# A gated Fourier and attention block: order and rooms of the last gates' side work, clearing of the score rooms, and where the output weights are prepared

## The chip, the cores and the metric
One core of a Trainium2 chip runs the whole block as one program. The metric is the device time of one execution in microseconds (us), here the median of three. The engines are TensorE (PE in the rows, PEld its weight loads), VectorE (DVE), ScalarE (ACT), GpSimd (POOL) and SyncE (SP), which issues most transfers (DMAs). Each takes its own instructions strictly in order.

## The reference
```python
D_MODEL, SEQ, CTX_LEN, NA_HEADS, HEAD_DIM = 1024, 2048, 256, 8, 64
WIN_ROWS, WIN_COLS, D_FF = 8, 16, 4096
...
def fourier_mix(u):
    ug = u.reshape(b, n, N_FOURIER_GROUPS, FOURIER_GROUP_DIM)          # 4 groups of 128 channels
    return jnp.fft.fft2(ug, axes=(1, 3), norm="ortho").real
...
        sc = jnp.concatenate([s_loc, s_ctx], axis=-1)                  # window of 8 x 16 and the 256 context keys
        p = jax.nn.softmax(sc, axis=-1)
...
def gated_merge(h, y_four, y_attn, w_gate, w_fo, w_ao, w_o):
    gates = jax.nn.sigmoid(h @ w_gate)
    g_f, g_a = jnp.split(gates, N_BRANCHES, axis=-1)
    merged = g_f * (y_four @ w_fo) + g_a * (y_attn @ w_ao)
    return merged @ w_o
```
Before it stand a normalisation with scale and shift (from c and c_ctx) and one projection of the tokens to f, q, k, v; behind it a residual, a second normalisation and a squared-ReLU MLP. All is float32 in the reference.

## The kernel before
Most products are made of float16 halves: a factor is split into a high part H and the rest L, and three matmuls (HH, HL, LH) add up in PSUM. Splitting takes one ScalarE pass and one VectorE pass (`pair_of`, L374/L375 or L847/L848 in the rows), or three POOL passes (`parts_on_pool`, L1429 to L1433).

The stages, with times from the trace: normalisation and first projections to about 140 us; pairs of projections (`run_pair`: f, gates, q, v, k) to about 849; the Fourier transform over the sequence (`psq`) to 886; attention with work beside it to about 1230; output projection (`po`) and the MLP to the end at 2648.

A scheduler places the instructions of each engine from the program's order and modelled times. Two things bind it: `tc.issue_after(i)` keeps what is built inside it behind instruction i, and a tile's room (a tag with `bufs` copies) is taken again only when its last reader is done. Generators are run piece by piece beside a main stream: `next(side)` builds one more piece.

**Last gates.** In the last pair (two gate units, matmuls `ps_g`, evictions `ot_g` on ScalarE, stores `gT`) the side generator is `fourier_prep`. It loads the four Fourier groups fT (tile X, 1 MB each), takes their squares' sum on ScalarE (L932, written into the `fold` tile), folds them on POOL and VectorE, adds the sum over partitions on TensorE (`pfe`), and makes the channel transform (`pc`, evicted to gH/gL). In between it loads 8 MB of weights for their norms (tiles wn, a 1 MB load each, ScalarE square L892; two of the norms, in weights of the Fourier output, are added up by matmul `pw`), and adds and splits two sets of rows of the Fourier output weights (wf, wx). `tick` hands out the pieces by a `pace`. After the gates, `pss`, `pr` and `puc` make the row of frequency 0, and `psq` transforms over the sequence; its results are split into y0H/y0L and y1H/y1L.

**Ramp of the attention.** Bias tiles bt are loaded by SP and POOL and scaled on POOL (L1194). A head's block runs score matmuls `sc`, a VectorE pass that adds the bias, writes s and takes the maximum m (L1347), ScalarE's exponential (L1351), transposes `tp`, a split into pH and pL (L1363, L1368), and `pv`. The four rooms s (128 x 832) are set to zero once, on POOL (L1268). Meanwhile `mgs` and `vsc` (scales of the merge, chains of small VectorE instructions around the matmuls `pym` and `pyb`) are made.

**Beside the attention and at its end.** Fillers run between blocks: `merge_fourier` (matmuls `pmf`, results stored to mF), then `load_wa` (the attention's output weights wa), then `attn_out(0, ...)`: loads of the attention's result (`yat`, split to yaH and yaL), matmuls `pua`, gate products in `ga` and `ft`, and the merged halves mH, mL. `output_weights` (generator `gating`) loads and converts wo on POOL. What is left over runs when the attention is done, `attn_out(1, ...)` included. The parts touched here are driven by these lines:
```python
        if n >= 8 and n % 2:
            with tc.issue_after(last_qk[0].ins):
                next(gating, None)
```


## Time and profile before
| what | value |
|---|---|
| median of 3 executions (lowest to highest) | 2649.96 us (2649.69 to 2651.73) |
| the profiled execution: its time, its span | 2649.84 us, 2648.1 us |
| mean granted TensorE clock | 0.985 |
| TensorE busy | 2518.0 us, 95% |
| VectorE, ScalarE, POOL busy | 1815.2, 1165.6, 475.5 us |
| mean DMA rate over the span | 191 GB/s |

The span is what the profile covers; the execution's own time is 1.74 us longer. Times in rows count from the span's start. A row of a timeline has start, duration, engine, line, operation, out<-in, shape, count (xN: neighbours joined), and in brackets the idle time of that engine before it with the instruction or transfer that ended it. Granted clock 1.00 is full speed of TensorE, 0.50 half.

### The profile page before, as it was taken

The page shows a single profiled execution, that of the slowest core. Times are in us where ns is not written, and L with a number is a line of the kernel's source. Part 1 is how long each engine was busy: PE and PEld are TensorE (multiplying, and loading weights), DVE is VectorE, ACT ScalarE, POOL GpSimd, SP SyncE. Part 2 cuts the span into 40 slices and gives each one's busy share as a digit, 9 for nine tenths or more (in the row PEclk, how much of TensorE's full clock was granted, in tenths as well). Part 3 has the DMA queues.
Part 4 walks back from the last instruction along what each step waited for, and adds up shares of the span by engine and source line. Part 5 has one row for each costly group of instructions (what it writes and reads, how often), then busy time and mean ns, then how long its engine had stood idle before and what let it go on. Part 6 is the DMA issues. An engine that isn't in the chain of part 4 may idle for free.

```text
span 2648.1 us, 42112 instructions
## 1 busy us (share of the span) xinstructions
PE 2518.0 (95%) x15839; PEld 1446.4 (55%) x15839; DVE 1815.2 (69%) x3730; ACT 1165.6 (44%) x2078; POOL 475.5 (18%) x587
## 2 busy tenths in 40 slices
PE   7899989899989599988999999999999999999999
PEld 5445757767745377876665444444444444444444
DVE  7656986685535488886776697979877644546367
ACT  5523226453243288883444564637361423314050
POOL 1201111012111664373000121121211100000000
PEclk9899999999989799999999999999999999999999
DMA  7456689763193655655667677786776533333334
GB/s 280 138 200 207 194 276 324 243 213 122 59 289 111 169 148 165 181 134 187 228 229 281 245 253 243 248 271 222 279 241 225 176 96 108 99 105 102 102 101 155
DMA packets 223196, 506.38 MB, mean 191 GB/s; under 512 B 31804, under 2 KB 85828, under 8 KB 207888
## 3 DMA queue, kind: packets, MB, share of 16 engines
q1 hardware_dynamic: 189936, 384.53, 45.3%
q0 software_dynamic: 26272, 87.95, 9.5%
q10 hardware_dynamic: 6784, 31.21, 3.5%
q8 instruction: 124, 2.03, 0.3%
q14 instruction: 80, 0.66, 0.1%
HBM read 366.22 MB, written 137.38 MB: 190 GB/s over the span
## 4 chain that ended last, share of the span: by engine, by line
PE 71%; DVE 10%; DMA 8%; issue 4%; POOL 3%; ACT 3%; SPq 0%; ACTq 0%; DVEq 0%; POOLq 0%
PE p L85 21%; PE pm L85 18%; PE ps_g L85 8%; PE po L85 6%; DMA w12m<-in_w_mlp 3%; PE pua L85 3%; PE ps_k L85 2%; PE tp L1360 2%; PE ps_f L85 2%; PE pmf L1298 2%; PE pv L1374 1%; PE sc L1338 1%; DVE wo L375 1%; PE ps_q L85 1%; DMA raw<-in_w_mlp 1%
## 5 line engine op out<-in xcount | busy, mean ns | idle before, releaser
L85 PE MATMUL pm<-hc,wb 128*128 128x512 f16 x2688 | 582.6, 379 | 5.7 <-DVE u L1652 3.5
L85 PE MATMUL p<-wb,a 128*128 128x512 f16 x2688 | 581.9, 379 | 2.1 <-DVE X L1652 1.5
L85 PEld LDWEIGHTS <-wb 128*128 128x128 f16 x2688 | 263.0, 98 | 323.6 <-issue 7.4
L85 PEld LDWEIGHTS <-a 128*128 128x128 f16 x2688 | 263.0, 98 | 319.7 <-issue 2.9
L85 PE MATMUL ps_g<-hx,w_g 128*128 128x512 f16 x1536 | 347.3, 383 | 1.0 <-DVE qn_q L563 1.0
L1652 DVE TENSOR_TENSOR X<-X,p 128x512 f32<-128x512 f32 x280 | 184.2, 684 | 171.3 <-PE p L85 152.1
L85 PEld LDWEIGHTS <-hx 128*128 128x128 f16 x2304 | 226.7, 99 | 37.7 <-issue 5.3
L85 PEld LDWEIGHTS <-w_g 128*128 128x128 f16 x1536 | 151.8, 100 | 170.8 <-issue 7.0
L85 PE MATMUL po<-wo,mH 128*128 128x512 f16 x512 | 152.4, 379 | 2.8 <-DVE ga L1418 2.8
L1652 DVE TENSOR_TENSOR u<-pm,u 128x512 f32<-128x512 f32 x128 | 87.5, 689 | 84.3 <-PE pm L85 82.5
L1347 DVE CUSTOM_DVE_ANT_0 s<-sc,bt,qsc 128x736 f32<-128x736 f32 (+5 forms) x128 | 111.2, 869 | 46.4 <-PE sc L1341 21.8
L374 ACT ACTIVATE wo<-ws,msc 128x512 f16<-128x512 f32 x96 | 69.0, 718 | 166.9 <-DVE ws L415 131.6
L1656 ACT ACTIVATE p<-pm 128x512 f32<-128x512 f32 x32 | 18.9, 590 | 239.7 <-PE pm L85 239.7
L1368 DVE SCALAR_TENSOR_TENSOR pL<-tp,pH 128x640 f16<-128x640 f32 (+1 forms) x128 | 112.3, 877 | 11.4 <-ACT pH L1363 10.7
L1351 ACT ACTIVATE s<-s,m 128x736 f32<-128x736 f32 (+5 forms) x128 | 104.4, 816 | 35.6 <-DVE m L1347 35.2
L1786 POOL DMA_DIRECT2D xr<-x1d x32 | 17.3, 540 | 569.2 <-DVE X L1652 562.6
L501 ACT ACTIVATE ot_g<-ps_g,usc_g 128x512 f32<-128x512 f32 x64 | 43.5, 682 | 152.9 <-PE ps_g L85 139.6
L374 ACT ACTIVATE wo<-raw,msc 128x512 f16<-128x512 f32 x128 | 87.5, 709 | 40.3 <-DVE raw L415 18.5
L1360 PE MATMUL tp<-ident,s 128*128 128x128 f32 x704 | 103.6, 282 | 0.9 <-ACT s L1351 0.8
L375 DVE SCALAR_TENSOR_TENSOR wo<-raw,msc,wo 128x512 f16<-128x512 f32 x128 | 94.4, 747 | 8.0 <-ACT wo L374 8.0
L85 PE MATMUL po<-wo,mL 128*128 128x512 f16 x256 | 97.0, 379 | 0.0
L85 PE MATMUL pua<-yaH,wa 128*128 128x256 f16 x512 | 87.2, 272 | 9.6 <-DVE ga L1418 4.4
(562 smaller groups left out, 4403.7 us busy)
## 6 DMA issues: line engine op xcount, KB each, us to landing
wb<-w1d SPq DMA_DIRECT2D x224, 256.0 KB
wb<-w2d SPq DMA_DIRECT2D x224, 256.0 KB
w12m<-in_w_mlp SPq DMA_DIRECT2D x32, 1024.0 KB
raw<-in_w_mlp ACTq DMA_DIRECT2D x24, 1024.0 KB
w1d<-wo POOLq DMA_DIRECT2D x84, 256.0 KB, 3.8
w2d<-wo POOLq DMA_DIRECT2D x84, 256.0 KB, 4.0
gT<-ot_g SPq DMA_DIRECT2D x64, 256.0 KB
hc<-hcd SPq DMA_DIRECT2D x14, 1024.0 KB
```

What stands on the lines that cost most here:

```text
L85: last_mm[0] = pe.matmul(ps, l, r, start=(start and i == 0), stop=(stop and i == n - 1))
L374: act.activation(hi, src, AF.Copy, scale=scale)
L375: dve.scalar_tensor_tensor(out=lo, in0=src, scalar=scale, in1=hi, op0=ALU.mult, op1=ALU.subtract)
L501: act.activation(o, ps, func, scale=scale)
L1298: pe.matmul(ps, l, r, start=(i == 0), stop=(i == len(prods) - 1))
L1338: pe.matmul(sc[:, lo:lo + nl], q, k[:, k0:k0 + nr * 64].rearrange("p (r c) -> p r c", c=64)[:, :, c0:c0 + ncl], start=(i == 0), stop=(i == 1))
L1347: tail["dve"] = dve.tensor_tensor_reduce(out=s[:, :n], in0=sc, in1=bias, op0=ALU.add, op1=ALU.min, scale=qsc[:, 4:5], scalar=3.0e38, accum ...
L1351: tail["act"] = act.activation(s[:, :n], s[:, :n], AF.Exp, bias=m1[:, 0:1], scale=-1.0, accum_out=m1[:, 1:2])
L1360: tail["pe"] = pe.transpose(tp[:, i * 128:(i + 1) * 128], s[:, o:o + 128], ident)
L1368: tail["dve"] = dve.scalar_tensor_tensor(out=pL[:, :c], in0=tp[:, :c], scalar=PTOP, in1=pH[:, :c], op0=ALU.mult, op1=ALU.subtract)
L1374: tail["pe"] = pe.matmul(pv, p_[:nk, i * 128:(i + 1) * 128], vv[:nk, h2 * 128 + o:h2 * 128 + o + 64], start=(j == 0 and i == 0), stop=(j = ...
L1652: last["dve"] = dve.tensor_tensor(out=o, in0=x, in1=y, op=op)
```

## The change
In the last gates `fourier_prep` is written out in one fixed order of steps. Its tiles become fixed rooms: two for the rows (both, mix), one for the weights whose norms are taken, and two for the Fourier groups, of which the first shares the tag of the gates' raw weights. The next norm load follows the square of the one before. In the last pair each step is kept behind the last gate eviction on ScalarE (`last_out`), and `pace` is 8 instead of 6. Three DMAs of four rows go from POOL's to SyncE's queue. The pieces `pss`, `pr`, `puc` come to lie between gate matmuls.

The score rooms are cleared by VectorE. The loads and conversions of wo leave the attention's main loop: two, later three steps follow the stores of each of merge_fourier's eight outputs. wa is split on ScalarE and VectorE out of tiles that held the Fourier results y; ft of the second row block is multiplied on POOL.

The old `fourier_prep` is among the functions printed above; of its removed lines the diff shows none.

```diff
     def tick(share):
 
         ticks[0] += pace[0]
-        with tc.issue_after(last_load[0].ins):
+        with tc.issue_after(last_load[0].ins), tc.issue_after(last_out[0].ins) if side not in beside else nullcontext():
             while ticks[0] >= 2:
                 ticks[0] -= 2
...
-        act.activation(o, ps, func, scale=scale)
+        last_out[0] = act.activation(o, ps, func, scale=scale)
...
-        pace[0] = 6 if n == len(seq) - 1 else (0, 3, 2)[min(n, 2)]
+        pace[0] = 8 if n == len(seq) - 1 else (0, 3, 2)[min(n, 2)]
...
-    folds, tabs, x_load = {}, [], []
-
-    def fold_load(g):
-        folds[g] = ff.tile([128, S], F32, tag="X", name=f"X{g}")
-        x_load.append(sp.dma_start(folds[g], fT[g]))
-
-    def fold(g, fo, eng=pool):
-        X = folds.pop(g)
+    folds, tabs, x_loads = {}, [], []
+
+    def fold(g, fo, X, eng=pool):
...
     def fourier_prep():
+        rooms = [pa.tile([128, 2, D], F32, tag="w", name=f"fw{i}", bufs=4) for i in range(2)]
+        norm_room, x_room = (pa.tile([128, 2, D], F32, tag="wst", name=f"fn{i}", bufs=2) for i in range(2))
+        x_rooms = (x_room.rearrange("p k n -> p (k n)"), ff.tile([128, S], F32, tag="X", name="X"))
+        loads, todo = iter((6, 7, 0, 1, 2, 3, 4, 5)), []
+        wf = a["w_fourier_out"][0]
+        both, mix = rooms
+        fos = []
 
         def norm_load():
             j = next(loads, None)
             if j is not None:
+                w, k = ((a["w_attn_out"][0], j), (a["w_out"][0], j - 2), (wf, j - 6))[(j >= 2) + (j >= 6)]
+                todo.append(j)
+                sp.dma_start(norm_room, w[k * 256:(k + 1) * 256, :].rearrange("(k p) n -> p k n", p=128))
 
         def norm():
+            j, tn = todo.pop(), norm_room.rearrange("p k n -> p (k n)")
             act.activation(tn, tn, AF.Square, accum_out=wn[:, j:j + 1])
+            norm_load()
+
+        def x_square(g):
+            fos.append(ff.tile([128, 4, 512], F32, tag="fold", name=f"fold{g}", bufs=2))
+            act.activation(fos[g].rearrange("p i t -> p (i t)"), x_rooms[g % 2], AF.Square, accum_out=fen[:, g:g + 1])
+
+        def x_load(g):
+            if g < 4:
+                x_loads.append(sp.dma_start(x_rooms[g % 2], fT[g]))
+
+        def x_sum(g):
+            spread(fpy[:, g:g + 1], fen[:, g:g + 1], f"pfe{g}")
+            pool.tensor_tensor(fpy[:, g:g + 1], fpy[:, g:g + 1], half[:, 0:1], op=ALU.pow)
+
+        def x_scale(g):
+            power_of_two(fpy[:, g:g + 1], HTOP, 1.0e-9)
+            dve.reciprocal(fup[:, g:g + 1], fpy[:, g:g + 1])
+            dve.tensor_scalar(out=fup[:, g:g + 1], in0=fup[:, g:g + 1], scalar1=GUP, scalar2=None, op0=ALU.mult)
+
+        def rows_load(p):
             w, wm = both[:, 0], both[:, 1]
             pool.memset(wm, 0.0)
             for h in range(2):
                 o, r0 = 64 * h, (2 * p + h) * 128
                 sp.dma_start(w[o:o + 64], wf[r0:r0 + 64, :])
                 sp.dma_start(wm[o + 1:o + 64], wfr[2 * p + h])
+
+        def rows_mix():
+            for x, op in enumerate((ALU.add, ALU.subtract)):
+                dve.tensor_tensor(out=mix[:, x], in0=both[:, 0], in1=both[:, 1], op=op)
+
+        def rows_split(p, x):
+            pair_of(*(t[:, p] for t in ws[x]), mix[:, x], iw)
+
+        def table(g):
+            t = fb.tile([128, 2, 4, 512], F16, tag=f"t{g}", name=f"t{g}")
+            sp.dma_start(t.rearrange("p o j m -> p (o j m)"), a["seq"][g])
+            tabs.append((t[:, 0], t[:, 1]))
+
+        x_load(0)
+        norm_load()
+        rows_load(0)
+        for _ in range(4):
             yield
...
+        norm()
+        yield
+        x_load(1)
+        x_square(0)
+        yield
+        norm()
+        yield
+        fold(0, fos[0], x_rooms[0])
+        x_load(2)
+        yield
+        x_sum(0)
+        spread(iw, wn[:, 6:7], "pw6")
+        spread(fsc[:, 23:24], wn[:, 7:8], "pw7")
+        dve.tensor_tensor(out=mgs[:, 9:10], in0=iw, in1=fsc[:, 23:24], op=ALU.add)
+        pool.tensor_tensor(mgs[:, 9:10], mgs[:, 9:10], half[:, 0:1], op=ALU.pow)
+        yield
+        x_scale(0)
+        dve.tensor_copy(iw, mgs[:, 9:10])
+        power_of_two(iw, HTOP / 2, 1.0e-9)
+        dve.tensor_copy(fsc[:, 23:24], iw)
+        dve.reciprocal(iw, iw)
+        rows_mix()
+        yield
+        rows_split(0, 0)
+        yield
+        rows_split(0, 1)
+        rows_load(1)
+        yield
+        yield from channel_dft(0)
+        norm()
+        table(0)
+        yield
+        x_square(1)
+        yield
+        fold(1, fos[1], x_rooms[1])
+        x_load(3)
+        yield
+        x_sum(1)
...
+        t = both[:, 0]
+        pool.memset(t, 0.0)
+        for o in (0, 32, 64):
+            sp.dma_start(t[o:o + 4], raw(wf, 64 * D, [[128 * D, 4], [1, D]]))
...
-        row = room("row")[0:1, 0]
+        row = mix[0:1, 0]
...
     for t in sts:
-        pool.memset(t, 0.0)
+        dve.memset(t, 0.0)
...
-                pool.dma_start(mF[m, :, h * 1024:(h + 1) * 1024], o[h])
+                i = pool.dma_start(mF[m, :, h * 1024:(h + 1) * 1024], o[h])
+            with tc.issue_after(i.ins):
+                for _ in range(2 if m < 2 else 3):
+                    next(gating, None)
...
-                eng.tensor_tensor(out=ft, in0=ft, in1=gf, op=ALU.mult)
+                (pool if t < 2 else dve).tensor_tensor(out=ft, in0=ft, in1=gf, op=ALU.mult)
...
     def load_wa():
+        raws = [py.tile([128, D], F32, tag=f"y{k // 2}{'HL'[k % 2]}", name=f"wao{k}") for k in range(4)]
         for k in range(4):
-            pool.dma_start(wa[:, k].rearrange("p n o t -> p (n o t)").bitcast(F32), a["w_attn_out"][0, k * 128:(k + 1) * 128, :])
-        yield
+            pool.dma_start(raws[k], a["w_attn_out"][0, k * 128:(k + 1) * 128, :])
+        for _ in range(6):
+            yield
         for k in range(4):
             for n_ in range(2):
-                parts_on_pool(wa, k, n_, None, f"wa{k}_{n_}")
-            yield
+                pair_of(wa[:, k, n_, 0], wa[:, k, n_, 1], raws[k][:, n_ * 512:(n_ + 1) * 512], mgs[:, 0:1])
+                yield
 
...
-            yield
+            if k % 2:
+                yield
-                parts_on_pool(wo, k, n, g1r, f"wt{k}_{n}")
+                t = py.tile([128, 512], F32, tag="wt", name=f"wt{k}_{n}")
+                pool.tensor_tensor(t, wo[:, k, n].rearrange("p o t -> p (o t)").bitcast(F32), g1r[:, n * 512:(n + 1) * 512], op=ALU.mult)
+                pool.tensor_copy(wo[:, k, n, 0], t)
+                pool.tensor_tensor(wo[:, k, n, 1], t, wo[:, k, n, 0], op=ALU.subtract)
                 yield
 
...
-        if n >= 8 and n % 2:
-            with tc.issue_after(last_qk[0].ins):
-                next(gating, None)
```

The order of the instructions, before and after, at three places. First SyncE's queue in the last gates: X (after: the first fn of fT) is a Fourier group, wn and fn weights for norms, wf and fw the rows.

Before:
```order
L887 DMA wn_8515<-in_w_out 128x2x1024
L902 DMA wf_8822<-in_w_fourier_out 64x1024
L609 DMA kHL<-sH_k_8169 64x2x512 x2
L609 DMA kHL<-sL_k_8170 64x2x512 x2
L502 DMA gT<-ot_g_0_8281 128x512
L887 DMA wn_8712<-in_w_out 128x2x1024
L903 DMA wf_8822<-in_w_fourier_rev 63x1024
L902 DMA wf_8822<-in_w_fourier_out 64x1024
L903 DMA wf_8822<-in_w_fourier_rev 63x1024
L887 DMA wn_8715<-in_w_out 128x2x1024
L1055 DMA chan<-in_chan 128x392
L820 DMA X_8284<-fT 128x2048
```
After:
```order
L897 DMA fn_8287<-fT 128x2048
L884 DMA fn_8286<-in_w_fourier_out 128x2x1024
L502 DMA gT<-ot_g_0_8073 128x512
L609 DMA kHL<-sH_k_7895 64x2x512 x2
L609 DMA kHL<-sL_k_7896 64x2x512 x2
L913 DMA fw_8284<-in_w_fourier_out 64x1024
L914 DMA fw_8284<-in_w_fourier_rev 63x1024
L913 DMA fw_8284<-in_w_fourier_out 64x1024
L914 DMA fw_8284<-in_w_fourier_rev 63x1024
L502 DMA gT<-ot_g_1_8201 128x512
L913 DMA fw_8284<-in_w_fourier_out 64x1024 x2
```
The first Fourier group's load, twelfth here before, now is the first of the loads, ahead of the first norm's. On ScalarE in the same place, before:
```order
L892 ACTIVATE wn_8512,wn<-wn_8512 128x2048
L892 ACTIVATE wn_8515,wn<-wn_8515 128x2048
L501 ACTIVATE ot_g_1_8338<-ps_g_1_8313,usc_g_7567 128x512
L892 ACTIVATE wn_8712,wn<-wn_8712 128x2048
L501 ACTIVATE ot_g_0_8377<-ps_g_0_8352,usc_g_7571 128x512
L892 ACTIVATE wn_8715,wn<-wn_8715 128x2048
L932 ACTIVATE fold_8291,fsc<-X_8284 128x2048
L501 ACTIVATE ot_g_1_8450<-ps_g_1_8425,usc_g_7571 128x512
```
After:
```order
L501 ACTIVATE ot_g_1_8321<-ps_g_1_8296,usc_g_7567 128x512
L888 ACTIVATE fn_8286,wn<-fn_8286 128x2048
L893 ACTIVATE fold_8327,fsc<-fn_8287 128x2048
L501 ACTIVATE ot_g_0_8375<-ps_g_0_8350,usc_g_7571 128x512
L501 ACTIVATE ot_g_1_8435<-ps_g_1_8410,usc_g_7571 128x512
L842 ACTIVATE gH_0_8438<-pc_0_8446,fsc 128x4x64
L842 ACTIVATE eH<-pc_0_8446,fsc 128x4
L842 ACTIVATE gH_1_8440<-pc_1_8455,fsc 128x4x64
L888 ACTIVATE fn_8286,wn<-fn_8286 128x2048
```
Four norm squares stood ahead of the first group's square within these rows; now one does, and the next norm square comes behind the first evictions of the channel transform.

Second, VectorE where the scores begin (ISA is the score pass, L1347 before, L1400 after). Before, from the scales of the merge to their first small instructions:
```order
L1107 TENSOR_REDUCE ymax<-A_2_9316 4x1
L1115 TENSOR_REDUCE mgs<-ymax 128x1
L1119 TENSOR_REDUCE mgs<-pym 2x1
L1120 TENSOR_SCALAR mgs<-ident,mgs 2x2
L1123 COPY mgs<-pyb 128x2
L1125 COPY vsc<-mgs 128x1
L1132 SCALAR_TENSOR_TENSOR mgs<-mgs 128x1
L246 TENSOR_SCALAR vsc<-vsc 128x1
```
After:
```order
L1165 TENSOR_REDUCE mgs<-ymax 128x1
L1169 TENSOR_REDUCE mgs<-pym 2x1
L1318 MEMSET s_9406 128x832
L1318 MEMSET s_9407 128x832
L1318 MEMSET s_9408 128x832
L1318 MEMSET s_9409 128x832
L1170 TENSOR_SCALAR mgs<-ident,mgs 2x2
L1400 ISA s_9406,m_0_0_9429<-sc_0_0_9424,bt_9336,qsc 128x520
L1400 ISA m_0_0_9429 128x1
L1173 COPY mgs<-pyb 128x2
L1175 COPY vsc<-mgs 128x1
```
The four memsets come in behind the reduce of pym, and the first score pass stands ahead of the small instructions. Before, all of these came ahead of the first pass. On POOL in the same place, before (the nine bias scalings and what follows):
```order
L1190 DMA bt_9355<-in_bias 128x2x288
L1459 DMA wo<-in_w_out 128x1024 x8
L1194 TENSOR_SCALAR bt_9349<-bt_9349,qsc 128x2x264
L1194 TENSOR_SCALAR bt_9349<-bt_9349,qsc 128x2x352
L1194 TENSOR_SCALAR bt_9349<-bt_9349,qsc 128x2x264
L1194 TENSOR_SCALAR bt_9352<-bt_9352,qsc 128x2x360
L1194 TENSOR_SCALAR bt_9352<-bt_9352,qsc 128x2x480
L1194 TENSOR_SCALAR bt_9352<-bt_9352,qsc 128x2x360
L1194 TENSOR_SCALAR bt_9355<-bt_9355,qsc 128x2x288
L1276 MEMSET s_9427 68x1024
```
After:
```order
L1240 DMA bt_9342<-in_bias 128x2x288
L1244 TENSOR_SCALAR bt_9336<-bt_9336,qsc 128x2x264
L1244 TENSOR_SCALAR bt_9336<-bt_9336,qsc 128x2x352
L1244 TENSOR_SCALAR bt_9336<-bt_9336,qsc 128x2x264
L1244 TENSOR_SCALAR bt_9339<-bt_9339,qsc 128x2x360
L1244 TENSOR_SCALAR bt_9339<-bt_9339,qsc 128x2x480
L1244 TENSOR_SCALAR bt_9339<-bt_9339,qsc 128x2x360
L1244 TENSOR_SCALAR bt_9342<-bt_9342,qsc 128x2x288
L1244 TENSOR_SCALAR bt_9342<-bt_9342,qsc 128x2x384
L1244 TENSOR_SCALAR bt_9342<-bt_9342,qsc 128x2x288
L1326 MEMSET s_9414 68x1024
L1338 COPY mo_1_9442<-uc 128x1
```
The eight weight loads ahead of the scalings are gone.

Third, VectorE near the end of the attention. Before, the output products' passes:
```order
L1367 RECIPROCAL ri_3_1_15219<-m_3_1_15131 128x1
L1418 SCALAR_TENSOR_TENSOR ga_0_14397<-pua_0_14404,mgs,ga_0_14397 128x256
L1419 SCALAR_TENSOR_TENSOR ga_0_14397<-ft_0_14399,mgs,ga_0_14397 128x256
L1421 TENSOR_TENSOR mL_14396<-ga_0_14397,mH_14395 128x256
L1418 SCALAR_TENSOR_TENSOR ga_0_14397<-pua_1_14462,mgs,ga_0_14397 128x256
L1419 SCALAR_TENSOR_TENSOR ga_0_14397<-ft_0_14399,mgs,ga_0_14397 128x256
L1421 TENSOR_TENSOR mL_14396<-ga_0_14397,mH_14395 128x256
```
After:
```order
L1420 RECIPROCAL ri_1_3_14574<-m_1_3_14465 128x1
L1421 SCALAR_TENSOR_TENSOR pL_1_3_14565<-tp_1_3_14557,pH_1_3_14564 128x768
L1471 SCALAR_TENSOR_TENSOR ga_0_14376<-pua_0_14383,mgs,ga_0_14376 128x256
L1472 SCALAR_TENSOR_TENSOR ga_0_14376<-ft_0_14378,mgs,ga_0_14376 128x256
L1400 ISA s_9407,m_2_0_14630<-sc_2_0_14625,bt_9339,qsc 128x616
L1400 ISA m_2_0_14630 128x1
L1420 RECIPROCAL ri_1_3_14632<-m_1_3_14516 128x1
L1421 SCALAR_TENSOR_TENSOR pL_1_3_14623<-tp_1_3_14615,pH_1_3_14622 128x768
L1474 TENSOR_TENSOR mL_14375<-ga_0_14376,mH_14374 128x256
L1471 SCALAR_TENSOR_TENSOR ga_0_14376<-pua_1_14441,mgs,ga_0_14376 128x256
```
What stood in one lump is now one product to a block, with score passes (ISA) between. Some 80 rows further up, the parts of wa now stand among the score passes:
```order
L1420 RECIPROCAL ri_3_1_13720<-m_3_1_13637 128x1
L843 SCALAR_TENSOR_TENSOR wa<-wao_13476,mgs,wa 128x512 x2
L1421 SCALAR_TENSOR_TENSOR pL_3_1_13711<-tp_3_1_13704,pH_3_1_13710 128x640
L1400 ISA s_9408,m_3_3_13764<-sc_3_3_13759,bt_9342,qsc 128x544
L1400 ISA m_3_3_13764 128x1
L1420 RECIPROCAL ri_3_2_13766<-m_3_2_13677 128x1
L843 SCALAR_TENSOR_TENSOR wa<-wao_13477,mgs,wa 128x512
L1421 SCALAR_TENSOR_TENSOR pL_3_2_13757<-tp_3_2_13750,pH_3_2_13756 128x640
```
Before, they were on POOL.

118 lines of the change are left out of this document (40 added, 78 removed).

## Prediction
> **What bounds the kernel now.** I read the page's busy times first, then TensorE's list of waits over the whole span, then the same list for the end of the attention, and last the timelines around the two longest waits. The columns of a list of waits are: total, times, longest.
>
> ```profile
> PE 2518.0 (95%) x15839; PEld 1446.4 (55%) x15839; DVE 1815.2 (69%) x3730; ACT 1165.6 (44%) x2078; POOL 475.5 (18%) x587
> ...
> PE sc L1338 <- DVE m L1347: 23.7, 4, 22.7
> PE pfe L872 <- ACT fold L932: 10.3, 1, 10.3
> ...
> PE pua L85 <- DVE ga L1418: 4.4, 5, 1.9
> PE pua L85 <- ACT yaH L1400: 4.3, 2, 4.0
> PE po L85 <- DVE ga L1418: 2.8, 1, 2.8
> PE ty L1385 <- DVE ga L1418: 2.7, 2, 1.7
> ```
>
> TensorE is busy for 95% of the span, so only its 130 us of idle time (2648.1 - 2518.0) are to be had, and the change touches three pieces of it: one wait of 10.3 us for the first Fourier table, one of 22.7 us ahead of the first scores, and some 15 us in small waits (the last four rows: 14.2) where the attention ends.
>
> **Last gates.** Columns: start, duration, engine, instruction, idle time before it and what ended it. The windows' row gives busy times, granted clock and the DMA engines' share.
>
> ```profile
> 743.15 25.20 PE L85 MATMUL ps_g<-hx,w_g 128*128 128x512 f16 x116
> 778.68 0.59 PE L872 MATMUL pfe<-fsc,ones 128*128 128x1 f32 x2 [10.33 <-ACT fold L932]
> 779.13 3.57 PE L85 MATMUL ps_g<-hx,w_g 128*128 128x512 f16 x8
> ...
> 766.13 1.91 ACT L892 ACTIVATE wn<-wn 128x2048 f32<-128x2048 f32 x1 [7.25 <-DMA wn<-in_w_out]
> 773.64 1.91 ACT L892 ACTIVATE wn<-wn 128x2048 f32<-128x2048 f32 x1 [4.92 <-DMA wn<-in_w_out]
> 776.62 1.91 ACT L932 ACTIVATE fold<-X 128x2048 f32<-128x2048 f32 x1 [0.98 <-DMA X<-fT]
> ...
> 720.16 7.45 SPq L887 DMA_DIRECT2D wn<-in_w_fourier_out  x2
> 760.83 0.66 SPq L820 DMA_DIRECT2D X<-fT  x1
> 804.47 0.33 SPq L820 DMA_DIRECT2D X<-fT  x1
> ...
> 725.20 1.91 ACT L892 ACTIVATE wn<-wn 128x2048 f32<-128x2048 f32 x1 [1.15 <-DMA wn<-in_w_fourier_out]
> 809.65 1.91 ACT L932 ACTIVATE fold<-X 128x2048 f32<-128x2048 f32 x1 [0.17 <-DMA X<-fT]
> ...
> 740.00:768.00 28.00, 28.00 (x133) 12.80 (x131) 2.85 (x4) 9.30 (x11) 0.95 (x1) 1.00 0.98 246
> ```
>
> TensorE stands at the pfe matmul from 768.35 on. It waits for ScalarE's square of X0, whose load SyncE issued only at 760.83, behind norm and row loads while the DMA engines were 0.98 busy; ScalarE, in order, stood at two norm loads in front of it. After the stall eight matmuls take 3.57 us instead of 8 x 0.217 (25.20/116) = 1.74: half speed. The fold's and the table's next pieces run at it too; I put the whole slow stretch at 3.0.
>
> The change issues X0 as the first of these loads, at 720, where a load of the same 1 MB was in use 5.0 us later (725.20 against 720.16). In the new order pfe comes after 28 + 58 = 86 gate matmuls from the same point where 22 + 116 = 138 stood, 52 x 0.217 = 11.3 us sooner, at 757.1. X0's square stands in ScalarE's queue behind one gate eviction and one norm square, about 752 to 754: no wait, with some 3 us to spare. What is late next is the second norm: its load now needs the one norm room to be free (754) and stands on SyncE behind X1 and two sequence tables of 1 MB each. Four MB at 246 to 400 GB/s, less what is through by then, land at 760 to 766; its square takes 1.91, and TensorE comes to the matmul that needs it at about 767. I charge 1.5 us for this and for two small waits at the second group. The three row DMAs that go from POOL's queue to SyncE's stand behind a gate store there; with 5.2 us from a quiet load's issue to its use (804.47 to 809.65) they are hidden by the group that follows. If that cover went, their reader, the last row split, would be late by those 5.2 us. Gate evictions behind a waiting norm cost nothing: in 740 to 768 TensorE was busy 28.00 of 28.00 while ScalarE waited up to 7.25. Sum: -10.33 - 3.0 + 1.5 = **-12** (from -5, if the second norm lands 7 us late, to -13.3).
>
> **The ramp.**
>
> ```profile
> 866.40 0.38 PE L85 MATMUL pr<-w0H,cH 128*1 128x512 f16 x1 [0.35 <-ACT row L1019]
> 872.21 0.75 DVE L848 SCALAR_TENSOR_TENSOR y0L<-A,fsc,y0H 128x512 f16<-128x512 f32 x1 [5.37 <-ACT y0H L847]
> 874.27 1.01 PE L85 MATMUL psq<-t,gH 128*128 128x512 f16 x2 [2.92 <-DVE y1L L848]
> 877.56 0.59 PE L85 MATMUL psq<-t,gH 128*128 128x512 f16 x2
> ...
> 877.07 0.57 POOL L1459 DMA_DIRECT2D wo<-in_w_out  x1
> 890.59 13.72 POOL L1194 TENSOR_SCALAR bt<-bt,qsc 128x528 f32<-128x528 f32 x7
> 910.40 2.98 POOL L1268 MEMSET s<- 128x832 f32 x4
> ...
> 888.42 0.28 DVE L1119 TENSOR_REDUCE mgs<-pym 2x1 f32<-2x128 f32 x1 [0.45 <-PE pym L1118]
> 890.27 1.04 DVE L1137 SCALAR_TENSOR_TENSOR mgs<-mgs,vsc 128x1 f32<-128x1 f32 x1
> 911.21 0.76 DVE L1347 CUSTOM_DVE_ANT_0 s<-sc,bt,qsc 128x520 f32<-128x520 f32 x1 [17.70 <-POOL s L1268]
> ...
> 912.04 0.62 PE L1338 MATMUL sc<-k,Q 128*128 128x264 f16 x2 [22.66 <-DVE m L1347]
> 912.88 0.63 PE L1298 MATMUL pmf<-y0H,w0H 128*128 128x512 f16 x1
> 918.69 0.38 PE L1298 MATMUL pmf<-y0L,w0H 128*128 128x512 f16 x1
> ...
> 851.40 0.75 DVE L977 TENSOR_SCALAR g1r<-g1r,mgs 128x1024 f32<-128x1024 f32 x1
> 1173.03 0.98 DVE L1347 CUSTOM_DVE_ANT_0 s<-sc,bt,qsc 128x736 f32<-128x736 f32 x1
> ```
>
> The first score pass waits 17.70 us for POOL's memsets of s, which stand in POOL's queue behind eight weight loads (issued from 877.07), all nine bias scalings (13.72 for seven, 1.96 each) and one weight product. The change puts the memsets on VectorE behind the reduce of 888.42, and the weight loads some rows of the merge later. The trace has no such memset on VectorE. Scaled from the two nearest rows it lies between 0.61 (0.75 x 832/1024) and 1.11 (0.98 x 832/736); neither is nearer, so I take the middle, 0.86, four times 3.4. By the Trainium skill, "VectorE: DVE Perf Modes", section "Zero memsets can be issued as uint32 (trn2)", a memset takes a cycle for each element, by estimate 0.87 us at that page's 0.96 GHz; the sum would not move.
>
> Before that the stage gets shorter: the 2.92 wait of psq came because two rows and uc stood ahead of y0H in ScalarE's queue; they now lie among the gate matmuls. With its slow restart (1.01 against 0.59, in all about 1.0) and 0.35 at the rows, less 0.6 for waits that the rows meet in their new place, that is 3.7. So the score pass starts at 888.42 + 0.28 + 3.4 + 0.2 - 3.7 = 888.6 instead of 911.2, if bias tiles are scaled by then: the weight loads no longer stand ahead, and three scalings from 877 end at 883. It hands TensorE its next scores some 22.6 us sooner. Against it go some twenty scalar instructions of the merge, which VectorE did during the idle time and which now stand between the first three passes, at 0.15 or, beside POOL's scalings, up to 1.04: half of them in TensorE's way, 2 us. **-20.6** (from -16, with memsets at 1.11, 3 us of scaling and the slow scalars, to -23).
>
> The restart at half speed (0.63 until 917.7, then 0.38) I leave as it is. The Trainium skill, "TensorE: Matmul & The Clock Gate", section "What's actually happening", has the clock fall after an idle window of about 3.4 us. By it a ramp whose single waits are shorter might stay at full speed, which is worth half of 5.7 us here: 2613 instead of the sum below. The trace speaks against it: a wait of 2.92 was followed by half speed.
>
> **End of the attention.**
>
> ```profile
> L375 DVE SCALAR_TENSOR_TENSOR wo<-raw,msc,wo 128x512 f16<-128x512 f32 x128 | 94.4, 747 | 8.0 <-ACT wo L374 8.0
> ...
> 1124.00:1130.00 6.00, 6.00 (x97) 5.58 (x95) 5.88 (x17) 5.98 (x16) 1.62 (x3) 1.00 1.05 341
> ...
> 1187.20 0.48 DVE L1419 SCALAR_TENSOR_TENSOR ga<-ft,mgs,ga 128x256 f32<-128x256 f32 x1
> 1199.27 0.48 DVE L1418 SCALAR_TENSOR_TENSOR ga<-pua,mgs,ga 128x256 f32<-128x256 f32 x1
> 1200.40 1.90 DVE L1419 SCALAR_TENSOR_TENSOR ga<-ft,mgs,ga 128x256 f32<-128x256 f32 x1
> ...
> 1200.75 1.27 POOL L1411 TENSOR_TENSOR ft<-ft,gf 128x512 f32<-128x512 f32 x1
> ```
>
> The eight parts of wa go from POOL to ScalarE and VectorE, at 0.75 each by the same form (L375): 6.0 us of VectorE in some seven steps where it is busy 5.88 of 6.00, and TensorE 6.00. Some slack is left: +5. In return the output products of the first rows can go one to each attention step instead of in a lump behind wa. Of the small waits, yaH's 4.3 stays (its store and load are not touched); of the other 4.4 + 2.7 + 2.8 = 9.9 about two thirds go: -6.5. The late weight conversions and ft's product on POOL cost nothing while VectorE has slack. **-1.5** (from -7 to +5).
>
> **Sum.** 2649.84 is the profiled execution's own time, 0.12 below the median shown. 2649.84 - 12 - 20.6 - 1.5 = 2615.7: **2616**.
>
> **Rivals.**
> *The ramp meets another wait.* If the first score pass has to wait for all nine bias scalings instead of three, it starts at 877.1 + 9 x 1.96 = 894.7, 6 us later; with memsets at 1.11 another 1.0. 2623. For it: the trace shows no landing time of the tiles that are scaled first, only that POOL came to them at 890.59; against it: the order puts the needed three first.
> *VectorE and POOL lock each other.* A pass that reads two SBUF tensors took 0.48 at 1187.20 and 1.90 at 1200.40 with POOL's product beside it, while the one that reads PSUM (1199.27) stayed at 0.48. The eight wa passes read two SBUF tensors. At half of 8 x 1.42 more, with TensorE waiting, C is +4.2: 2621 to 2622. The Trainium skill, "SBUF — State Buffer", section "Who interferes with whom", says that such an instruction contends with a GpSimd that reads SBUF; by that rule, the trace agrees (0.48 against 1.90).
> *The first stall only moves* to the second norm or second table: A is 0 to -2, about 2626.
> *Slower.* One norm room makes a chain of load, square, load; if the X loads fall behind it on SyncE, each of the four pfe waits as the first did: 4 x 10.33 - 10.33 = 31 us more. 2649.84 + 31 - 22.1 = 2659. The next pfe come 58 to 70 gate matmuls (12.6 to 15.2 us) apart, so it decides at about 11 us from issue to landing, 13 less the square; the quiet load had 5.2.
>
> **How the numbers follow.** All three parts as summed: 0.58 (2607 to 2621). Another ramp wait: 0.13. Lock: 0.13. Stall moved: 0.09. Slower: 0.03. That the change does not do what it says is left: the order shows the memsets and loads moved, so 0.04, spread around no change. The range 2606 to 2632 takes in all but the last two, the low end with the clock case, the high one with two rivals half true. A measurement of this kernel tells 0.2% (5.3 us) from no change: faster 0.93, same 0.04, slower 0.03.
>
> **What would show it.** pfe without a wait above 2 us and no half clock behind it; psq without its 2.92; VectorE's memset row at 0.6 to 1.1 and the score pass behind it within 5 us of the reduce; the wait of sc below 7; wa's passes at 0.75 with TensorE idle some 5 us there; yaH's wait still about 4. The prediction is wrong if the score pass then waits for POOL's scalings, if pw or a later pfe waits for a norm or X load, or if the wa passes take over 1 us.

## The result and the profile after

The changed kernel took 2610.63 us (median of 4 runs, 2606.54 to 2615.99) against 2649.82 for the kernel before in the same comparison (2646.87 to 2651.73): ratio 0.9854, 95% interval 0.9831 to 0.9877. That is 39 us faster; forecast were 34. The profiled execution took 2607.65 us with a span of 2605.9, 42.2 less than before.

Four landmarks split the 42.2: the last but one `tq_k` (after it the last gates begin), the last `psq` matmul, the first score pass (the first L1347 before, L1400 after), the first `mo` (VectorE's first output of merge_fourier) and the first `po`.

| stretch | before, us | after, us | difference | predicted |
|---|---|---|---|---|
| start to `tq_k` (code not changed) | 737.96 | 739.73 | +1.8 | 0 |
| to the last `psq`: gates, rows | 148.0 | 131.8 | -16.2 | -12 - 3.7 = -15.7 |
| to the first score pass: ramp | 25.25 | 6.79 | -18.5 | -18.9 |
| to the first `mo` | 17.5 | 17.1 | -0.4 | +2 |
| to the first `po`: attention and its end | 301.1 | 291.9 | -9.2 | -1.5 |
| to the end (code not changed) | 1418.3 | 1418.6 | +0.3 | 0 |

The list of TensorE's waits over the span (total, times, longest) and the line of busy times, after:

```profile
PE 2512.3 (96%) x15839; PEld 1445.3 (55%) x15839; DVE 1814.5 (70%) x3738; ACT 1169.0 (45%) x2086; POOL 449.9 (17%) x560
...
PE pyb L1172 <- DVE mgs L1170: 3.9, 1, 3.9
...
PE pym L1168 <- DVE mgs L1165: 1.8, 1, 1.8
...
PE pua L85 <- ACT yaH L1453: 1.3, 1, 1.3
```

The 10.3 of pfe and the 22.7 of sc have left the list, and of the 9.9 us of waits for ga 0.3 are left. TensorE's busy time fell too, by 5.7 us (2518.0 to 2512.3), with the same 15839 matmuls: fewer of them run at half clock behind a long wait, and the mean granted clock rose from 0.985 to 0.992.

**Last gates, after.** Timeline rows:

```profile
721.93 0.33 SPq L897 DMA_DIRECT2D fn<-fT  x1
...
752.83 1.90 ACT L893 ACTIVATE fold<-fn 128x2048 f32<-128x2048 f32 x1
...
758.73 0.28 PE L867 MATMUL pfe<-fsc,ones 128*128 128x1 f32 x2
...
805.43 1.08 PE L856 MATMUL pc<-chan,fold 128*128 128x64 f32 x8 [2.00 <-DVE eL L843]
```

The first Fourier group's load is issued at 721.93 (760.83 before), its square stands at 752.83, and pfe, 20 us earlier than before, waits for nothing. What is late next is small: 2.00 us for `pc` of the third group.

**Ramp, after.** Timeline rows of POOL, VectorE and TensorE, and one row of busy times (PE, PEld, DVE, ACT, POOL; granted clock; DMA share; GB/s):

```profile
854.38 17.56 POOL L1244 TENSOR_SCALAR bt<-bt,qsc 128x528 f32<-128x528 f32 x9 [12.02 <-DMA bt<-in_bias]
...
874.60 0.28 DVE L1169 TENSOR_REDUCE mgs<-pym 2x1 f32<-2x128 f32 x1 [0.45 <-PE pym L1168]
875.00 3.37 DVE L1318 MEMSET s<- 128x832 f32 x4
...
878.32 0.74 DVE L1400 CUSTOM_DVE_ANT_0 s<-sc,bt,qsc 128x520 f32<-128x520 f32 x1
...
878.46 0.58 PE L1172 MATMUL pyb<-mgs,ones 2*128 2x2 f32 x2 [3.89 <-DVE mgs L1170]
879.12 0.62 PE L1391 MATMUL sc<-k,Q 128*128 128x264 f16 x2
...
879.00:883.00 4.00, 3.92 (x17) 2.67 (x17) 2.88 (x23) 2.35 (x5) 1.33 (x3) 0.50 0.00 0
```

The four memsets take 3.37 on VectorE (predicted 3.4), and the score pass starts 3.7 us behind the reduce. All nine bias scalings are through at 871.9, before the memsets begin. Where TensorE waited 22.66 us it now waits 1.84 and 3.89 (pym, pyb) and then runs at half clock for some 4 us.

**End of the attention.** Rows of busy times from the first `mo` to the first `po`, first before, then after; the last row is the stretch in which wa is split:

```profile
928.70:1229.80 301.10, 282.40 (x3636) 230.46 (x3635) 257.91 (x560) 236.51 (x533) 168.76 (x160) 0.99 0.56 163
```

```profile
895.40:1187.30 291.90, 280.19 (x3637) 229.85 (x3635) 256.55 (x567) 239.34 (x542) 155.66 (x155) 1.00 0.63 182
...
1091.00:1120.00 29.00, 23.78 (x328) 20.46 (x327) 28.48 (x61) 27.47 (x65) 21.35 (x20) 1.00 0.81 208
```

Of the 9.2 us, 7.0 are idle time of TensorE (18.7 to 11.7), 2.2 are matmuls that no longer run slowly. In the stretch of wa TensorE stands 5.2 us: the charge of +5 is there in this profile (how much of it is the split's is looked at below). More than it comes back in the waits behind: those for ga and yaH's. That chain before (store of yA, its load yat, split, matmul):

```profile
1149.05 0.33 ACTq L1388 DMA_DIRECT2D yA<-yo  x1
1153.67 0.40 SPq L1157 DMA_DIRECT2D yat<-yA  x1
...
1158.15 1.06 ACT L1400 ACTIVATE yaH<-yat 128x1024 f16<-128x1024 f32 x1 [3.71 <-DMA yat<-yA]
1159.26 0.27 PE L85 MATMUL pua<-yaH,wa 128*128 128x256 f16 x1 [4.00 <-ACT yaH L1400]
...
1160.00:1164.00 4.00, 3.91 (x38) 3.30 (x34) 2.14 (x5) 2.88 (x9) 3.93 (x4) 0.57 0.69 151
```

and after:

```profile
1123.63 0.33 ACTq L1441 DMA_DIRECT2D yA<-yo  x1
1126.17 0.39 SPq L1207 DMA_DIRECT2D yat<-yA  x1
...
1130.05 1.06 ACT L1453 ACTIVATE yaH<-yat 128x1024 f16<-128x1024 f32 x1 [1.03 <-DMA yat<-yA]
1131.15 0.27 PE L85 MATMUL pua<-yaH,wa 128*128 128x256 f16 x1 [1.31 <-ACT yaH L1453]
```

From the issue of the store to that of the load it is 4.6 us before and 2.5 after; TensorE's wait falls from 4.00 to 1.31, and the stretch of granted clock 0.57 behind it is gone. SyncE issues the load as soon as the store has landed (1153.53 before, 1126.03 after). In this step the DMA engines were 0.71 busy before and 0.34 after. The second profile of the changed kernel (below) has 4.05 us for the step, a DMA share of 0.46 and a wait of 2.90: so the wait fell in both, by 1.1 to 2.7 us, but its size changes from one execution to the next.

### The profile page after: what moved, and what is told of

Same layout as the page of the kernel before. It is cut to its first block, busy times and chain, and to the rows that moved or that the text cites. A ratio compares the mean times of both kernels' runs of the same rounds, so it can differ in the third digit from the quotient of the medians.

```text
span 2605.9 us, 42107 instructions
## 1 busy us (share of the span) xinstructions
PE 2512.3 (96%) x15839; PEld 1445.3 (55%) x15839; DVE 1814.5 (70%) x3738; ACT 1169.0 (45%) x2086; POOL 449.9 (17%) x560
## 4 chain that ended last, share of the span: by engine, by line
PE 71%; DMA 11%; DVE 10%; ACT 4%; issue 3%; POOL 1%; SPq 1%; ACTq 0%; DVEq 0%; POOLq 0%
PE p L85 21%; PE pm L85 19%; PE ps_g L85 8%; PE po L85 5%; DMA w12m<-in_w_mlp 3%; PE ps_k L85 3%; PE pua L85 2%; PE tp L1413 2%; PE ps_f L85 2%; PE pv L1427 2%; PE pmf L1348 1%; DMA vt<-v 1%; PE sc L1391 1%; DVE wo L375 1%; PE ps_q L85 1%
## 5 line engine op out<-in xcount | busy, mean ns | idle before, releaser
L1400 DVE CUSTOM_DVE_ANT_0 s<-sc,bt,qsc 128x736 f32<-128x736 f32 (+5 forms) x128 | 111.1, 868 | 22.4 <-PE sc L1394 16.8
L1701 ACT ACTIVATE p<-pm 128x512 f32<-128x512 f32 x32 | 18.9, 589 | 239.7 <-PE pm L85 239.7
L1421 DVE SCALAR_TENSOR_TENSOR pL<-tp,pH 128x640 f16<-128x640 f32 (+1 forms) x128 | 112.3, 878 | 11.8 <-ACT pH L1416 11.0
L1416 ACT ACTIVATE pH<-tp 128x640 f16<-128x640 f32 (+1 forms) x128 | 95.8, 748 | 0.5 <-PE tp L1413 0.5
```

The source lines that it names most:

```text
L1400: tail["dve"] = dve.tensor_tensor_reduce(out=s[:, :n], in0=sc, in1=bias, op0=ALU.add, op1=ALU.min, scale=qsc[:, 4:5], scalar=3.0e38, accum ...
L1416: tail["act"] = act.activation(pH[:, :c], tp[:, :c], AF.Copy, scale=PTOP)
L1421: tail["dve"] = dve.scalar_tensor_tensor(out=pL[:, :c], in0=tp[:, :c], scalar=PTOP, in1=pH[:, :c], op0=ALU.mult, op1=ALU.subtract)
```

## The experiments

Each part was first put alone into the kernel before; then the ramp and wa, but not the gates, were taken out of the changed kernel. Ratios are to the kernel before on the same chip, with 95% intervals.

**The gates alone.** All of the change but the memsets, the output weights, wa and ft:

```diff
-        pace[0] = 6 if n == len(seq) - 1 else (0, 3, 2)[min(n, 2)]
+        pace[0] = 8 if n == len(seq) - 1 else (0, 3, 2)[min(n, 2)]
...
     def fourier_prep():
+        rooms = [pa.tile([128, 2, D], F32, tag="w", name=f"fw{i}", bufs=4) for i in range(2)]
...
```


> The kernel before with the first part alone (the last gates' order and rooms). Theory 1, the parts add up: the gates stall and psq's wait go, 16 us, and the wait ahead of the first scores stays about 22.7; about 2634. Theory 2, POOL's queue of the ramp starts when the matmul pss is through (its bias memset waited for pss until 859.9 before, until 832.1 after the whole change), so this part by itself pulls the bias loads, the scalings and POOL's memsets forward: the wait of sc falls to 8 to 12, and the time to about 2620 to 2624.

2641.07 us, 0.9943 (0.9925 to 0.9961): less gain than either theory gave. Counted from `tq_k`, the last `psq` comes 13.4 us earlier, and POOL's queue starts earlier too, but a new wait eats part of it. Timeline rows of ScalarE:

```profile
888.54 0.52 ACTq L1156 DMA_DIRECT2D y<-A  x1
889.11 0.68 ACT L1155 ACTIVATE A<-psq,fsc 4x512 f32<-4x512 f32 x1 [12.19 <-DMA Q<-qHL]
```

ScalarE's own store y<-A is issued only when another transfer, the second Q load on SyncE's queue, has landed; the split of A stands behind it in order, then VectorE's maxima, then TensorE's pym (12.4 us). The Q load was late because POOL now issued the 4 MB of wo 24.7 us sooner (852.39 instead of 877.07), into the same stretch as SyncE's loads of k, Q, vt.

The store and the Q load share no data. The trace's records show what ties them: both count up the same completion semaphore (number 107), and ahead of the store ScalarE waits on it until 888.47, when the Q load of 882.88 has landed. In this program the transfers of SyncE and ScalarE share eight such semaphores, and in this stretch an issue that waits does so for the transfer that used its semaphore before. In the kernel before, the store's semaphore had last served a load of vt, which had landed at 876.84, before the store was ready (885.37). So the new order of the gates made this dependency, and the early weights made it late.

**VectorE's memsets alone.**

```diff
-        pool.memset(t, 0.0)
+        dve.memset(t, 0.0)
```


> The kernel before with the four memsets of s on VectorE alone; here they come behind the small merge instructions. Theory 1, the first pass needs only the three scalings of its own bias tile (end about 896.5) and the memsets (3.4 us from 893.5): it starts at 897 instead of 911.2, 14 us less, about 2636. Rival, it needs all nine scalings (end near 909): 2 to 4 us less, about 2647.

2648.36 us, 0.9989 (0.9979 to 0.9999). That is the rival's time, but not for its reason: counted from the last `psq`, the score pass came 14.8 us earlier, as in theory 1, but the first `mo` only 5.2; the wait that ate the rest was in neither theory. Rows of TensorE, ScalarE and POOL:

```profile
917.88 0.32 PE L1374 MATMUL pv<-vt,pH 96*128 96x64 f16 x3 [9.84 <-ACT yp L1377]
```

```profile
916.58 1.06 ACT L1281 ACTIVATE a<-s 68x1024 f16<-68x1024 f32 x1 [9.72 <-DMA s<-y]
...
913.13 1.65 POOL L1278 DMA_DIRECT2D s<-y  x3
```

ScalarE stands in order at the split of frequency 0's row, whose load POOL issues at 913.13, behind the weight loads and scalings that had held the memsets. The stall only moved.

**The late weights alone.**

```diff
-                pool.dma_start(mF[m, :, h * 1024:(h + 1) * 1024], o[h])
+                i = pool.dma_start(mF[m, :, h * 1024:(h + 1) * 1024], o[h])
+            with tc.issue_after(i.ins):
+                for _ in range(2 if m < 2 else 3):
+                    next(gating, None)
...
-        if n >= 8 and n % 2:
-            with tc.issue_after(last_qk[0].ins):
-                next(gating, None)
```


> The kernel before with the output weights' loads and conversions moved behind merge_fourier's stores; memsets of s stay on POOL. Theory 1: POOL comes to its nine scalings at 877 instead of 890.6, its memsets end near 899, and the first score pass starts there instead of at 911.2: 12 us less, about 2638. Rival: the bias tiles have not landed at 877 (after the whole change POOL waited 12.0 for them), the scalings start at 885 or later, and only 4 to 6 us are gained, about 2645.

2639.24 us, 0.9948 (0.993 to 0.9966), theory 1: the pass comes 11.8 us behind psq instead of 25.25, and what it waits for is again POOL's memset, now behind scalings alone:

```profile
897.35 0.76 DVE L1350 CUSTOM_DVE_ANT_0 s<-sc,bt,qsc 128x520 f32<-128x520 f32 x1 [2.85 <-POOL s L1268]
```

**The ramp alone** (the last two edits together).

> The kernel before with the memsets of s on VectorE and the output weights late, both at once. Theory, each alone runs into what the other removes (the memsets alone: TensorE waited 9.8 us behind s<-y, whose load stood behind the weights on POOL; late weights alone: POOL's memsets held the first pass until 11.8 us after psq): both at once keep the first pass 10.5 us after psq, have no 9.8 wait behind it, and the part up to the first mo is 14 to 15 us shorter than before; with the shorter end of the attention 16 to 18 in all, about 2635. Rival, the two are independent and add up to what the single ones gave from the end of the projections, 10.4 + 2.8 = 13, and no more.

2643.38 us, 0.9968 (0.9957 to 0.998). The 9.8 us wait is gone and the first `mo` comes 14 us earlier, as forecast; but at the end 8.4 are left by the medians, less than the 16 to 18 of the theory and the 13 of the rival, and no more than the late weights gave alone (13.7). The list of waits:

```profile
PE pv L1377 <- ACT yp L1380: 5.1, 4, 3.9
PE po L85 <- DVE ga L1421: 3.9, 1, 3.9
```

The late conversions put three POOL passes for each of 16 pieces where POOL also splits wa. From the first `mo` to `po` it took 303.7 us (301.1 before), and from `po` to the end, where no code changed, 1421.1 (1418.3 before). Each difference is below what one profile can tell (see the changed kernel again, below), so where the rest went stays open.

**wa alone.**

```diff
-                parts_on_pool(wa, k, n_, None, f"wa{k}_{n_}")
+                pair_of(wa[:, k, n_, 0], wa[:, k, n_, 1], raws[k][:, n_ * 512:(n_ + 1) * 512], mgs[:, 0:1])
```


> The kernel before with wa split on ScalarE and VectorE and ft of the second row block on POOL; the output weights stay where they were. Theory 1: TensorE loses about 5 us beside the eight wa passes and gains the lump behind wa (10 of waits on ga) and some of yaH's 4.0: 7 to 9 us less, about 2642. Rival: POOL's weight conversions, which here stay beside them, lock more of the wa passes (2.1 instead of 0.73), and little is left: 0 to 3 us, about 2648.

2635.38 us, 0.9933 (0.9919 to 0.9948): 17.6 by the medians and 12.6 by the landmarks, more than was expected. No wait for ga and none for POOL is left, and yaH's is smaller:

```profile
PE pua L85 <- ACT yaH L1400: 1.6, 1, 1.6
```

All eight VectorE passes took 0.73 to 0.75; one of them ran beside a bias scaling of POOL (1133.70 to 1135.80) and was not held. The edit moves wa and the product ft together; no run takes the two apart.

**The changed kernel again**, to see how far an identical program's stretches move.

> The changed kernel once more. Theory: the spread of its times (2606 to 2616) comes from the unchanged projections between 300 and 600 us, so from the last k transposes but one to the end the profile repeats 1866 us within 2, and the median lies between 2606 and 2616. Rival: the new waits of the change differ between executions, and this length moves by 4 us or more.

2609.35 us, 0.9841 (0.9818 to 0.9864), 2603.43 to 2622.22 in five runs. The median lies where the theory put it, but the length from `tq_k` to the end, which it wanted within 2 us of 1866, was 1871.3, so there the rival is right. The gates took 1.9 us more than in the first trace, and from `mo` to `po` it was 295.2 instead of 291.9. So a stretch of one profile is good to some 3 us, and no smaller difference is read as an effect below.

**The changed kernel with POOL's memsets**

```diff
-        dve.memset(t, 0.0)
+        pool.memset(t, 0.0)
```


> The changed kernel with the four memsets back on POOL. Theory 1: since the weight loads are gone POOL is through with its scalings 2 us before the reduce of pym, so the memsets would end there 1.5 us behind it, where VectorE needs 3.4: pyb's wait of 3.9 falls to about 0.6, the first pass starts 2 us sooner, and 2 us are gained (2608 by the median shown). Theory 2, the prediction's: the memsets on POOL held up the scores, so POOL's queue makes them late again, and 5 us or more are lost.

2608.78 us, 0.9831 (0.9817 to 0.9845): no difference to the changed kernel. That rules out theory 2. The 2 us of theory 1 are too small for these times to tell, but its reason is not there: the pass starts 7.46 behind psq, not sooner than 6.79.

```profile
872.37 2.98 POOL L1318 MEMSET s<- 128x832 f32 x4
```

With the weight loads gone from its queue POOL is done with the memsets at 875.3. VectorE uses the time for the small merge instructions, which then stand ahead of the first pass instead of behind it; they make up for the 3.37. Which engine clears the rooms makes no measurable difference here.

**The split of wa two steps earlier**

```diff
-        for _ in range(6):
+        for _ in range(4):
```


> The changed kernel with four empty steps instead of six ahead of the splitting of wa. Theory, VectorE's passes over two SBUF tensors are held by POOL's: two of the eight wa passes took 2.08 and 1.34 because POOL scaled a bias tile and converted weights beside them; two steps sooner POOL only issues transfers there, all eight take 0.73, and TensorE's idle time in this stretch falls from 5.2 to about 3.2. Rival: TensorE waits there because VectorE and ScalarE have no slack at all, so the place changes nothing (5.2 again).

2609.22 us, 0.9825 (0.9808 to 0.9842): no difference. POOL's scaling moved with it, and two of the eight passes were still held (2.96 us for the two), so this run by itself does not tell the price. Another trace does: in the second profile of the changed kernel all eight passes took 0.73 to 0.76. Busy times of the 29 us that begin 9 us ahead of the first wa pass, in the first and in the second profile of the changed kernel (columns as above):

```profile
1083.88:1112.88 29.00, 23.61 (x330) 20.21 (x329) 28.51 (x61) 27.50 (x64) 19.57 (x18) 1.00 0.89 257
```

```profile
1083.71:1112.71 29.00, 25.70 (x358) 21.99 (x357) 28.31 (x65) 28.80 (x68) 15.90 (x15) 1.00 0.89 248
```

TensorE stands 5.4 us with two passes held and 3.3 with none; with POOL's memsets and with wa alone, where no pass was held either, it is 3.3 as well. So the theory's 3.2 is what these traces show: the split itself goes with 3.3 us of idle time, and being held by POOL adds about as much as it lengthens the passes (2.0 us). At the end of the program 2 us cannot be told.

**The changed kernel without the new ramp**

```diff
-        dve.memset(t, 0.0)
+        pool.memset(t, 0.0)
...
-            with tc.issue_after(i.ins):
-                for _ in range(2 if m < 2 else 3):
-                    next(gating, None)
...
+        if n >= 8 and n % 2:
+            with tc.issue_after(last_qk[0].ins):
+                next(gating, None)
```


> The changed kernel with the ramp undone (s cleared on POOL, wo loads and conversions back in the attention's main loop); gates and wa as changed. Theory 1 (the 18.5 us that the rows show between psq's end and the first score pass arrive in full at the end): psq's end to first score pass 25 us instead of 6.8, time 2628 us. Theory 2 (part of it is given back later, as with the ramp alone, which gained 14 at the first merge but 8.7 at the end): 2618 to 2620 us. The sum of the parts run alone (-13.7 for the gates, -12.6 for wa) lies between: 2652 - 26 = 2626.

2619.37 us, 0.9869 (0.9848 to 0.9891): theory 2 by the time. The pass comes 21.0 us behind psq, but the stretch from `mo` to `po` is one of the shortest (288.2). The hold is that of the gates alone. SyncE's and ScalarE's rows:

```profile
854.10 22.03 SPq L1207 DMA_DIRECT2D vt<-v  x16
...
882.10 0.52 ACTq L1156 DMA_DIRECT2D y<-A  x1
882.67 0.68 ACT L1155 ACTIVATE A<-psq,fsc 4x512 f32<-4x512 f32 x1 [11.96 <-DMA Q<-qHL]
```

and the changed kernel's for comparison:

```profile
851.62 12.36 SPq L1207 DMA_DIRECT2D vt<-v  x16
...
871.99 0.52 ACTq L1156 DMA_DIRECT2D y<-A  x1
```

Sixteen issues of vt take 22.03 us of SyncE instead of 12.36 while wo's 4 MB are in flight, so the second Q load, which stands behind them, goes out at 876.8 instead of 865.4, and ScalarE's store waits until it has landed. What SyncE waits for on the way are the transfers that had the semaphores of the vt loads before, bias loads above all. Its list of waits from 840 to 885 us (total, times, longest), without the new ramp and then in the changed kernel:

```profile
SPq L1207 <- DMA bt<-in_bias: 8.0, 3, 4.5
```

```profile
SPq L1207 <- DMA bt<-in_bias: 1.4, 3, 0.7
```

**The changed kernel with early weights**, VectorE's memsets kept (the edit above without its first two lines).

> The changed kernel with wo's loads and conversions back in the attention's main loop; s is cleared on VectorE. Theory 1 (early weight loads on POOL's queue hold the first load s<-y behind them, as with VectorE's memset alone): the first score pass stays 7 to 10 us behind psq, but pv waits 8 to 10 us for yp, and the time is 2618 to 2620 us. Theory 2 (the new gates have emptied POOL's queue and the DMA engines early enough): no wait over 4 us for yp, 2609 to 2612 us.

2620.72 us, 0.9878 (0.9863 to 0.9892): theory 1's time, but not for its reason. No wait for yp is over 0.4; the pass stands 21.1 behind psq, with VectorE's memsets on time behind a late reduce:

```profile
885.18 0.68 ACT L1155 ACTIVATE A<-psq,fsc 4x512 f32<-4x512 f32 x1 [11.92 <-DMA Q<-qHL]
```

So once the gates are changed the gain of the ramp that can be measured hangs on moving the weights, and none on the memsets. Loads and conversions of the weights were moved together; that it is the loads is read from the rows of SyncE.

**The changed kernel with wa on POOL**

```diff
-                pair_of(wa[:, k, n_, 0], wa[:, k, n_, 1], raws[k][:, n_ * 512:(n_ + 1) * 512], mgs[:, 0:1])
+                parts_on_pool(wa, k, n_, None, f"wa{k}_{n_}")
```


> The changed kernel with wa on POOL again and ft as before; gates and ramp as changed. Theory 1 (what the rows show from 1187 to 1230, and no more): +9.2 us, 2619 us, with yaH's wait of about 4 and the three ga waits (some 10 us together) back. Theory 2 (with the wo conversions late, wa's three POOL passes stand in one queue with them, so the parts collide): +13 to +18, 2623 to 2628 us, with a wait of pua for POOL's wa over 2.5 us.

2624.95 us, 0.988 (0.9848 to 0.9912): theory 2's time (28.7 us below the kernel before, where the changed kernel is 39 to 42 below), but pua waits for POOL's wa only 1.04 us at most. The price stands elsewhere. Rows of TensorE (one of them of busy times) and ScalarE:

```profile
1136.39 0.37 PE L1427 MATMUL pv<-vt,pH 128*128 128x64 f16 x4 [3.81 <-ACT yp L1430]
...
1206.39 0.59 PE L85 MATMUL po<-wo,mH 128*128 128x512 f16 x2 [3.89 <-DVE ga L1471]
...
1136.00:1142.00 6.00, 5.61 (x53) 5.06 (x53) 2.76 (x5) 4.73 (x12) 5.89 (x5) 0.50 0.48 103
```

```profile
1135.08 1.06 ACT L1453 ACTIVATE yaH<-yat 128x1024 f16<-128x1024 f32 x1 [3.32 <-DMA yat<-yA]
```

ScalarE waits for yat with yp behind it, TensorE waits 3.81 for yp and runs at half clock for 6 us. In five of the six kernels with wa on POOL this load costs TensorE one wait of 3.8 to 5.3 us, seen at yaH or at yp (before 4.00, gates alone 5.3, late weights 4.16, ramp alone 3.95, this one 3.81; memsets alone 1.7); in the eight profiles with wa split on ScalarE and VectorE the wait at yaH is 1.0 to 2.9.

**Four steps of wo instead of three behind the later outputs**

```diff
-                for _ in range(2 if m < 2 else 3):
+                for _ in range(2 if m < 2 else 4):
```


> The changed kernel with four instead of three steps of wo behind each of merge_fourier's later outputs, so that the conversions are through before wa is split. Theory 1 (the late conversions cost TensorE: from the first mo to the first po the changed kernel took 291.9 and 295.2 us, and 288.2 and 287.9 with the conversions early): from mo to po 288 to 290 us, all wa passes at 0.73 to 0.75, 2604 to 2608 us. Theory 2 (these few us come from how the attention's passes happen to fall, not from wo): 292 to 295 us, 2608 to 2613 us.

2610.42 us, 0.9841 (0.9819 to 0.9863), theory 2's time; 290.0 us from `mo` to `po`, theory 1's stretch, but no difference that stands out of the 3 us. The last conversion still ended at 1121.9 (1123.1 in the changed kernel), so conversions that are through early were not reached, and what the late ones cost stays open. No version tried is faster than the changed kernel.

## Why the prediction was right

The two long waits that the prediction named went, and the range held the time. That the sum came out within 5 us is in part luck, since two terms were mis-sized in opposite directions. Put alone into the kernel before, the three parts gave 11.9 (gates), 8.4 (ramp) and 17.6 us (wa) by the medians, together 37.9 of the 39 to 42 measured. Forecast for them were 15.7 (with psq's 3.7), 16.9 and 1.5, together 34.1: by these runs the ramp was put some 8 too high and the end of the attention some 16 too low.

**Last gates: right.** Predicted with psq's part -15.7, measured -16.2 in the profile shown and -14.3 in the second one; alone -13.4. pfe has no wait, no half clock behind it, and psq has lost its 2.92. The second norm, charged with 1.5 us, did not wait; a 2.00 at `pc` took its place.

**Ramp: right at the first score pass, about half of it at the end, and for a reason that was only half of the cause.** The memsets were sized right (3.37 for 3.4), and a pass 3.7 us behind the reduce is the term as worked out. By the Trainium skill, "VectorE: DVE Perf Modes", section "Zero memsets can be issued as uint32 (trn2)", one memset was estimated at 0.87; the trace agrees with 0.84 (3.37/4). The 2 us for small merge instructions did not show (0.15 to 0.20 each, beside a wait of 1.18), and the half clock behind the wait was shorter, 3.8 us instead of 5.7, with waits of 3.89 and 22.66 ahead of it. What the prediction did not see is that the memsets are exchangeable: it took POOL's memset row for the hold, but alone its removal gave 0.0011 of the time and in the changed kernel its return cost nothing. The weight loads in the same stretch are what holds: in POOL's queue before; once the gates are changed, by transfers that land later, SyncE's issues that wait for them, and the semaphore that ScalarE's store shares with the second Q load. Both edits were in the change, so the first score pass came where it was forecast. As the changed kernel is, the ramp is worth some 5 to 10 us at the end (without it, or with early weights alone, 34.3 and 32.9 us are left of the 39 to 42), not the 18.5 of the landmarks: without it the stretch from `mo` to `po` is 4 to 7 us shorter. Why that stretch gives part of it back stays open.

**End of the attention: the term that was mis-sized.** The step that failed is "yaH's 4.3 stays (its store and load are not touched)" with "about two thirds" of the ga waits. Measured: yaH's 4.3 became 1.3 (2.9 in the second profile), the ga waits went from 9.9 to 0.3, and 2.2 us of half clock went with them: -9.2 instead of -1.5, although TensorE stood 5.2 us beside the split, as charged. The store and load of yA were not touched by the edit, but they share the DMA engines and queues with what the edit moves; that this sets the wait is read from the shorter step at a lower DMA share (4.6 us at 0.71, 4.05 at 0.46, 2.5 at 0.34), and no run changes that traffic alone. That the edit as a whole is worth it is shown twice: put alone into the kernel before it gave 17.6 us, and without it the changed kernel takes 10 to 14 us more.

**Rivals.** Another ramp wait: no, all scalings were done in time. The stall only moved: not at pfe; it did just that for the memsets alone. Slower through the one norm room: no. VectorE and POOL locking each other: the mechanism is there, but its price is 2 us. Rows of VectorE and POOL:

```profile
1100.00 0.73 DVE L843 SCALAR_TENSOR_TENSOR wa<-wao,mgs,wa 128x512 f16<-128x512 f32 x1
...
1105.70 2.08 DVE L843 SCALAR_TENSOR_TENSOR wa<-wao,mgs,wa 128x512 f16<-128x512 f32 x1
```

```profile
1105.92 1.29 POOL L1509 TENSOR_TENSOR wt<-wo,g1r 128x512 f32<-128x512 f32 x1
1107.17 2.20 POOL L1244 TENSOR_SCALAR bt<-bt,qsc 128x576 f32<-128x576 f32 x1
```

One pass beside two of POOL's took 2.08 where its like took 0.73, and a pair beside a scaling of 2.62 took 2.07 instead of 1.40: 2.0 us in all, where the rival had half of 11.4. In the second profile of the same program no pass was held, though one ran beside a scaling (1104.84 to 1105.59, the scaling 1104.82 to 1107.46); so running beside POOL is not enough, and what decides is open. Two of the prediction's own signs came out against it: wa passes over 1 us (in one of the two profiles) and yaH's wait, which was to stay at about 4.

The range of 2606 to 2632 held the time; the forecast of 2616 lay 5 us above it, which is what the two errors leave of each other.
